# RWKV stage of a two-block model: both pairs of heads taken through every stage together, with smaller buffers beside it

## The chip, the cores and the metric

The kernel runs on one core of one Trainium2 chip. The metric is the device time of one execution in microseconds (us); before the change it was 2177.82 us as the median of three runs (2176.29 to 2183.47).

## The reference, cut to what matters

The program computes two transformer-like blocks. The first takes x (512 tokens, 1024 channels), norms it, projects it to four mixers of 256 channels (forgetting attention "fox", stick-breaking attention "stick", RWKV-7 time mix, gated linear recurrence "lru"), scales each by the silu of a gate, multiplies by an output matrix and adds the result to x. The second block has two layers whose norms are modulated by columns computed from a condition vector (`silu(c) @ w_ada + b_ada`).

The RWKV mixer has four heads of 64 channels. In the reference it is a scan over tokens:

```
def step(state, inp):
    r_t, w_t, k_t, v_t, kk_t, a_t = inp
    sa = jnp.einsum('bhij,bhj->bhi', state, -kk_t)
    state = (state * w_t[:, :, None, :]
             + sa[..., None] * (kk_t * a_t)[:, :, None, :]
             + v_t[..., None] * k_t[:, :, None, :])
    return state, jnp.einsum('bhij,bhj->bhi', state, r_t)
...
y = ((y - mean) * lax.rsqrt(var + GN_EPS)).reshape(b, s, G) * ln_g + ln_b
bonus = jnp.sum(r * k * r_k, axis=-1, keepdims=True) * v
return y + bonus.reshape(b, s, G)
```

## The kernel before, in words

Engines: TensorE (PE) multiplies, VectorE (DVE) and ScalarE (ACT) work on vectors, GpSimd (POOL) helps, SyncE (SP) issues the DMAs. All of them work through their own instructions in a fixed order.

**First block.** `first_block` (L403) norms x and splits the result into two float32r parts hH and hL (one buffer each, L389 to L393), which all projections read. A chunk of weights is loaded as raw tile `wr` (three buffers of 128x1024, 512 KB), copied by ACT to `wh` (L149) and subtracted by DVE to `wl` (L150); two buffers each. `proj_a` (L167) then makes three matmuls per step of 128 channels (L178, L179, L182). The steps are traced in the order of `B_ORDER`: `sq` (q, k, v of stick), `rw` (all of RWKV), `st` (stick), `fq` (q, k, v of fox), `lr`, three gates, `ad` (the modulation columns of the first layer, `ada`, L926), `fo` (fox, L523) and `g0`, the gate of fox.

**RWKV.** `rwkv` (L572) projects r, k, v and the low-rank features, and calls `rwkv_pair` (L635) for heads 0 and 1, then for heads 2 and 3. A pair computes operands, their transposes, Gram matrices over four blocks of 128 tokens (L731), the inverse of a triangular matrix by six doublings (`prod`, L756 to L783; each doubling of a head is three products of eight small matmuls, L761, with a copy and two subtractions of DVE between), parts that don't depend on the state, four state steps (L819 to L846) and a group norm. Its single-buffer tiles (`ar`, `gb`, `gk`, `up`, `cu`, `cl`) make the second pair wait for the first.

**Modulation columns.** `ada` multiplies 12 groups of 512 outputs by two vectors: 96 loads of 256 KB into tiles `wa` of their own (four buffers), four matmuls each (L938), and per group one copy to `row` (ACT), one transpose by the identity (PE) and one add (DVE, L945). The group's PSUM bank `ad` is single.

**After the mixers.** `out_split` (L1138) splits the mixers' output y into hH and hL again, in the very buffers that held the parts of x, and multiplies (L1154 to L1156). The second block follows, with tables of rope loaded into tiles `rcs` and `rsn` in the memory that the first block's working tiles held.

**What sets the order.** The framework orders each engine's instructions when the program is built: code traced earlier has priority, an instruction takes a place as soon as the framework's own estimate sees its inputs and a free buffer, and lower priorities fill the gaps. The lanes `rw`, `at`, `qkv`, `wa` have as many buffers as `B_LANES` says.

```
B_LANES = dict(rw=18, at=5, qkv=9, wa=4)
```

Of the kernel before, what the change touches and what calls it, by code (L numbers as in the profile page):

```python
# [16 lines left out]
P = 128  # L17
D = 1024
# [24 lines left out]
B_LANES = dict(rw=18, at=5, qkv=9, wa=4)  # L43
# [27 lines left out]
class Stream:  # L71
    """A run of n tokens (the latents or the context) with its buffers."""
# [7 lines left out]
class Kern:  # L80
# [41 lines left out]
    def t2(self, n=512):  # L122
        """A [128, n <= 512] float32 working tile of the current lane."""
# [29 lines left out]
    def weights(self, dram, nk):  # L153
        """Two halves of the chunk, each (H, L)."""
# [89 lines left out]
    def rstd_small(self, ss, scale, eps, post=1.0):  # L244
        """ss: SBUF [128, m]; returns post * (ss*scale + eps)^-1/2."""
# [10 lines left out]
    def consts(self):  # L256
        """What the scalar engine's tables are needed for comes first."""
# [8 lines left out]
        # 8 softplus(-lambda) of the recurrence, negated: 8 (ln sigmoid|lambda| - max(-lambda, 0))  # L266
# [6 lines left out]
        # silu of the conditioning vectors, as 32 columns  # L273
# [32 lines left out]
    def add_sq(self, s, k, key="ss", scale=1.0, first=None):  # L306
        """Adds the squares of channel tile k, scaled, to a sum of the stream's."""
# [8 lines left out]
    def mean_sq(self, s, sums):  # L316
        """Mean over the channels + eps, of each token: [128, token tile]."""
# [8 lines left out]
    def spread(self, s, r):  # L326
        """[128, token tile] to one row of all tokens on every partition."""
# [38 lines left out]
    def xy(self, s):  # L366
        """The residual stream and the mixers' output take turns in one buffer."""
# [15 lines left out]
    def res(self, s, d):  # L383
        """The residual of channel tile d, read back."""
# [15 lines left out]
# ======================================================================================  # L400
# first block
# ======================================================================================
    def first_block(self, s, con, filler):  # L403
        nc, a = self.nc, self.a
        with self.phase("b1", dict(rw=3, at=2, ad=1), B_LANES):
# [12 lines left out]
            steps = dict(rw=self.rwkv, ad=filler, fq=lambda: v.update(f=self.qkv(0, 1, 2)), fo=lambda: self.fox(v["f"]),  # L418
                         sq=lambda: v.update(s=self.qkv(4, 5, 6)), st=lambda: self.stick(v["s"]), lr=self.lru,
# [4 lines left out]
        # output projection and residual, with the norm of the context beside it  # L424
# [56 lines left out]
    def gates(self, which):  # L481
        """Scales rows of y by silu of the gate projections."""
# [8 lines left out]
    def qkv(self, cq, ck, cv):  # L491
# [12 lines left out]
    def flip(self, p, nk, tag):  # L504
        """[q, keys] -> [keys, (kt) q]."""
# [7 lines left out]
    def pv_pair(self, pts, vals, g, out, grid=None, tag="at"):  # L513
        """out [(head, d), q] of heads 2g and 2g+1 from their weights [keys, (kt) q]."""
# [57 lines left out]
    def rwkv(self):  # L572
# [7 lines left out]
        # triangular masks [128, 2, 128]; of the diagonal's 64 blocks [128, 64]: per level, and the identity  # L580
# [7 lines left out]
        lora = self._ld(work, "lora", [P, 2 * G])  # L588
# [13 lines left out]
        def ev_low(j, s, acc):  # L602
# [3 lines left out]
            else:  # L606
                # forget gates: cumulative log sigmoid, negated, as two float32r rows per head
# [27 lines left out]
    def rwkv_pair(self, hp, r, k, v, low, lora, gmask, lmask):  # L635
        nc = self.nc
        work = self.work
        col = lambda key: self.col1(key, hp)
        t4 = lambda t: t.rearrange("p (b t) -> p b t", b=4)
        big = lambda tag, dt=F32, bufs=1: work.tile([P, 8, P], dt, name=self.nm(tag), tag=tag, bufs=bufs)  # L640

        # removal key
# [6 lines left out]
        # 1/sqrt(max(ss, 1e-12))  # L649
# [4 lines left out]
        # decay: log decay = -exp(-1/2) sigmoid(w0 + tanh(wl) w2), cumulated within each block  # L654
# [29 lines left out]
        # replacement key  # L684
# [6 lines left out]
        # bonus  # L691
        bon = self.t2()
# [5 lines left out]
        # operands with the decays folded in  # L698
        ar = work.tile([P, 4, 2, P], F32, name=self.nm("ar"), tag="ar", bufs=1)
# [8 lines left out]
        # token-major copies  # L708
# [8 lines left out]
        tk = lambda key, h, b: tok[key][:, b * P + h * 64 : b * P + h * 64 + 64]  # L717

        # Gram matrices [s, t] by (head, block): beta.alpha (s<t), beta.rho, kappa.alpha (s<t), kappa.rho
        gb = work.tile([P, 8, 2, P], F32, name=self.nm("gb"), tag="gb", bufs=1)  # L720
        gk = big("gk")
        z = self.t2().rearrange("p (b h i) -> p b h i", b=4, h=2)
        gm = lambda n: gmask.rearrange("p (o a) t -> p o a t", o=1).to_broadcast([P, n, 2, P])
        for h in range(2):
            c = slice(h * 64, h * 64 + 64)
            ga = t4(self.t2())
            for src in (be, ka):
                for b in range(0, 4, 2):
# [4 lines left out]
                    u = slice(4 * h + b, 4 * h + b + 2)  # L733
                    if src is be:
                        nc.vector.tensor_tensor(gb[:, u], g, gm(2), ALU.mult)
                    else:
                        for o, m in ((ga[:, b : b + 2], 0), (gk[:, u], 1)):
                            nc.vector.tensor_tensor(o, g[:, :, m], gmask[:, m : m + 1].to_broadcast([P, 2, P]),
                                                    ALU.mult)
# [1195 lines left out]
```

## Time and profile before

| | |
|---|---|
| runs shown, median (lowest to highest) | 2177.82 us (2176.29 to 2183.47) |
| profiled execution, first to last instruction | 2176.9 us; the page gives no time around it |
| PE busy, share of the span | 2058.9 us, 95% |
| DVE, ACT, POOL busy | 1296.8, 993.4, 189.3 us |
| DMA | 221.95 MB, 102 GB/s over the span |
| mean granted clock of PE | 0.976 |

Matmuls are pipelined, so a busy PE is not a PE at its peak; and an engine's idle time matters only where nothing else holds the end. The first block ends where the first L1154 starts, at 395.89 us.

### The profile page before, as it was taken

What the parts mean: (1) busy time and instruction counts of PE and PEld (TensorE: products, weight loads), DVE (VectorE), ACT (ScalarE), POOL (GpSimd) and SP (SyncE); (2) the same over time, 40 slices, a digit from 0 to 9 for tenths busy, and PEclk for the clock granted to TensorE, in tenths of its full rate; (3) what the DMA queues carried; (4) which work ended last, traced back from release to release, by engine and by line L of the source; (5) the groups of instructions that cost most, each with busy time, mean ns of one, the idle gap of its engine ahead of it and who ended that gap; (6) DMA issues with size and microseconds to landing.
All of it is one profiled execution on the core that took longest, in us unless ns stands there. A gap on an engine that the chain in (4) does not pass through costs nothing.

```text
span 2176.9 us, 31989 instructions
## 1 busy us (share of the span) xinstructions
PE 2058.9 (95%) x12676; PEld 1669.3 (77%) x12676; DVE 1296.8 (60%) x2279; ACT 993.4 (46%) x1875; POOL 189.3 (9%) x148
## 2 busy tenths in 40 slices
PE   7999999978999899899999999989988989999999
PEld 5877766778957766788888888879957757787887
DVE  5354453676645575768885444677665656554544
ACT  4343743544756854542231323455656644242432
POOL 1011010032001000600000000161010001000000
PEclk9999999988999999999999999999999999999999
DMA  6323344332101124335673112434211222232232
GB/s 221 120 69 108 103 123 131 114 102 78 49 25 59 59 88 159 117 96 158 218 228 103 60 49 97 129 116 131 81 35 54 76 91 70 89 100 92 79 115 87
DMA packets 87622, 221.95 MB, mean 102 GB/s; under 512 B 13744, under 2 KB 24752, under 8 KB 87344
## 3 DMA queue, kind: packets, MB, share of 16 engines
q1 hardware_dynamic: 87472, 219.90, 31.6%
q8 instruction: 100, 1.64, 0.3%
q14 instruction: 50, 0.41, 0.1%
HBM read 212.53 MB, written 7.34 MB: 101 GB/s over the span
## 4 chain that ended last, share of the span: by engine, by line
PE 75%; DVE 13%; ACT 5%; DMA 4%; issue 2%; SPq 0%; POOL 0%; DVEq 0%; ACTq 0%; POOLq 0%
PE ps L178 15%; PE ps L182 14%; PE ps L179 14%; PE ps L203 3%; PE ps L202 3%; PE ps L204 3%; DVE wl L150 2%; DMA wr<-in_wadaT 2%; PE ps L1417 2%; PE ps L1154 2%; PE ps L1155 2%; PE ps L1156 2%; PE ps L397 2%; PE ps L1408 1%; PE ps L519 1%
## 5 line engine op out<-in xcount | busy, mean ns | idle before, releaser
L178 PE MATMUL ps<-hH,wh 128*128 128x512 f32 (+1 forms) x1424 | 511.2, 364 | 14.9 <-ACT wh L149 12.1
L179 PE MATMUL ps<-hL,wh 128*128 128x512 f32 (+1 forms) x1424 | 499.5, 360 | 1.4 <-DVE hL L363 0.7
L149 ACT CAST wh<-wr 128x1024 fp32r<-128x1024 f32 (+4 forms) x302 | 284.2, 943 | 464.1 <-PE ps L179 380.4
L150 DVE TENSOR_TENSOR wl<-wr,wh 128x1024 fp32r<-128x1024 f32 (+4 forms) x266 | 288.2, 1086 | 254.3 <-ACT wh L149 243.6
L182 PE MATMUL ps<-hH,wl 128*128 128x512 f32 (+1 forms) x1248 | 430.9, 369 | 2.8 <-DVE wl L150 2.8
L178 PEld LDWEIGHTS ps<-hH,wh 128*128 128x128 f32 x1424 | 271.5, 191 | 68.0 <-ACT wh L149 13.5
L179 PEld LDWEIGHTS ps<-hL,wh 128*128 128x128 f32 x1424 | 271.6, 191 | 43.6 <-issue 1.9
L182 PEld LDWEIGHTS ps<-hH,wl 128*128 128x128 f32 x1248 | 222.1, 188 | 39.5 <-DVE wl L150 4.8
L203 PE MATMUL ps<-wl,hH 128*128 128x256 f32 x704 | 203.2, 290 | 12.3 <-DVE wl L150 12.3
L202 PE MATMUL ps<-wh,hH 128*128 128x256 f32 x704 | 203.4, 291 | 0.2 <-ACT wh L149 0.2
L204 PE MATMUL ps<-wh,hL 128*128 128x256 f32 x704 | 200.6, 287 | 0.0
L178 PE MATMUL ps<-uH,wh 128*128 128x512 f32 (+1 forms) x528 | 187.7, 362 | 6.3 <-ACT uH L149 4.0
L179 PE MATMUL ps<-uL,wh 128*128 128x512 f32 (+1 forms) x528 | 181.6, 357 | 0.4 <-DVE uL L150 0.4
L182 PE MATMUL ps<-uH,wl 128*128 128x512 f32 (+1 forms) x488 | 155.4, 365 | 1.5 <-DVE wl L150 1.3
L203 PEld LDWEIGHTS ps<-wl,hH 128*128 128x128 f32 x704 | 137.4, 195 | 15.6 <-DVE wl L150 14.4
L202 PEld LDWEIGHTS ps<-wh,hH 128*128 128x128 f32 x704 | 136.7, 195 | 4.3 <-issue 2.9
L204 PEld LDWEIGHTS ps<-wh,hL 128*128 128x128 f32 x704 | 136.4, 195 | 1.0 <-issue 0.7
L1660 DVE SCALAR_TENSOR_TENSOR xy<-ps,mod,xy 128x512 f32<-128x512 f32 (+1 forms) x96 | 60.8, 658 | 128.1 <-PE ps L182 124.9
L150 POOL TENSOR_TENSOR wl<-wr,wh 128x1024 fp32r<-128x1024 f32 (+1 forms) x36 | 84.1, 2342 | 605.8 <-ACT wh L149 598.1
L178 PEld LDWEIGHTS ps<-uH,wh 128*128 128x128 f32 x528 | 99.4, 189 | 33.2 <-ACT wh L149 7.2
L179 PEld LDWEIGHTS ps<-uL,wh 128*128 128x128 f32 x528 | 99.7, 189 | 16.0 <-DVE uL L150 0.8
L145 ACT COPY t<-ps 128x512 f32<-128x512 f32 (+4 forms) x127 | 61.9, 490 | 89.7 <-PE ps L397 34.3
(364 smaller groups left out, 3276.4 us busy)
## 6 DMA issues: line engine op xcount, KB each, us to landing
wr<-in_up SPq DMA_DIRECT2D x110, 512.0 KB, 3.5
wa<-in_wada SPq DMA_DIRECT2D x96, 256.0 KB, 3.2
wr<-in_wadaT SPq DMA_DIRECT2D x48, 512.0 KB, 4.3
wr<-in_win2b SPq DMA_DIRECT2D x36, 512.0 KB, 3.5
wr<-in_win SPq DMA_DIRECT2D x30, 512.0 KB, 3.8
wr<-in_dn SPq DMA_DIRECT2D x40, 320.0 KB, 2.9
wr<-in_dn SPq DMA_DIRECT2D x32, 384.0 KB, 3.1
wr<-in_wout SPq DMA_DIRECT2D x12, 512.0 KB, 4.0
```

Source lines behind the costliest of these rows:

```text
L145: self.nc.any.tensor_copy(out, in_)
L149: self.nc.scalar.copy(hi, src)
L150: (eng or self.nc.vector).tensor_tensor(lo, src, hi.bitcast(F32), ALU.subtract)
L178: nc.tensor.matmul(acc[s], wh, fh(k), start=(q == 0), stop=False)
L179: nc.tensor.matmul(acc[s], wh, fl(k), start=False, stop=False)
L182: nc.tensor.matmul(acc[s], wl, fh(k), start=False, stop=(q == nk - 1))
L202: nc.tensor.matmul(bank[:, i], fh(k), wh, start=start, stop=False)
L203: nc.tensor.matmul(bank[:, i], fh(k), wl, start=False, stop=False)
L204: nc.tensor.matmul(bank[:, i], fl(k), wh, start=False, stop=stop)
L397: self.nc.tensor.transpose(out, in_, self.ident[:k, :k])
L1154: nc.tensor.matmul(acc, wh, yH[:, k], start=(q == 0), stop=False)
L1660: nc.vector.scalar_tensor_tensor(s.x[:, d, :], acc, self.mcol(5, d, s), s.x[:, d, :], ALU.mult, ALU.add)
```

## The change

RWKV no longer runs pair after pair. `rwkv_pair` is cut into `rwkv_operands`, `rwkv_gram`, `rwkv_inverse`, `rwkv_free`, `rwkv_block` and `rwkv_finish`, and each stage is traced for both pairs before the next; a doubling goes over four heads. To hold that, `ar` gets two buffers and `gb` four, and the lane `rw` 29 tiles in place of 18 tiles and several special ones. Space comes from elsewhere: the q of both attentions lies in rows of the output y that the mixer fills later, the bonus in y as well, the lane `qkv` falls from nine tiles to five and `at` from five to four, and `ada` loads its weights into the raw weight tiles `wr`, two steps of k at a time (48 loads of 512 KB), which it shares with all projections. What is computed stays the same.

```diff
-B_LANES = dict(rw=18, at=5, qkv=9, wa=4)
+B_LANES = dict(rw=29, at=4, qkv=5)
...
-        qt, kt, v = ([self.t2() for _ in range(2)] for _ in range(3))
+        kt, v = ([self.t2() for _ in range(2)] for _ in range(2))
+        qt = [self.y[:, row + j, :] for j in range(2)]
...
-        for hp in range(2):
-            self.rwkv_pair(hp, fs["r", hp], fs["k", hp], fs["v", hp], low["t"], lora, gmask, lmask)
...
+        pairs = [dict(hp=hp, r=fs["r", hp], k=fs["k", hp], v=fs["v", hp]) for hp in range(2)]
+        for d in pairs:
+            self.rwkv_operands(d, low["t"], lora)
+        for d in pairs:
+            self.rwkv_gram(d, gmask)
+        self.rwkv_inverse(pairs, lmask)
+        for d in pairs:
+            self.rwkv_free(d)
+        for b in range(4):
+            for d in pairs:
+                self.rwkv_block(d, b)
+        for d in pairs:
+            self.rwkv_finish(d)
...
-        bon = self.t2()
+        bon = self.y[:, 4 + hp, :]
...
-        for l in range(6):
-            for h, us in enumerate(hs):
+            for gb, up, cuh, clh, gd in heads:
...
-            for k in range(KT):
-                w = self.work.tile([P, 512], F32, name=self.nm("wa"), tag="wa", bufs=self.lanes["wa"])
-                self.dma(w, a["wada"][g, k])
-                for j in range(4):
+            for k0 in range(0, KT, 2):
+                w = self.wtile("wr")
+                self.dma(w.rearrange("p (k c) -> p k c", k=2), a["wada"][g, k0 : k0 + 2].rearrange("k p c -> p k c"))
+                for i in range(2):
+                    k = k0 + i
+                    for j in range(4):
```

Before, SP's queue in the middle of the first block reads as follows; `wr<-in_win` is a chunk of projection weights, `wa<-in_wada` one of modulation weights.

```order
L138 DMA wa_3014<-in_wada 128x512
L138 DMA wr_2330<-in_win 128x1024
L138 DMA wr_2388<-in_win 128x1024
L138 DMA wa_3020<-in_wada 128x512
L138 DMA wa_3026<-in_wada 128x512
L138 DMA wr_2394<-in_win 128x1024
L138 DMA wr_2452<-in_win 128x1024
L138 DMA wa_3032<-in_wada 128x512
```

In the changed program SP's queue holds no modulation weights until the weights of `g6`, the last gate but one, are issued; the place where they begin is this.

```order
L138 DMA wr_2728<-in_win 128x1024
L138 DMA wr_2790<-in_win 128x1024
L138 DMA wr_2796<-in_win 128x1024
L138 DMA wr_2862<-in_wada 128x2x512
L138 DMA wr_2872<-in_wada 128x2x512
L138 DMA wr_2882<-in_wada 128x2x512
L138 DMA t_3838<-in_xT 128x512
L138 DMA t_3860<-in_xT 128x512
```

From here on 48 loads of `in_wada` stand in a row, broken only by reads of x (`in_xT`), and the gate `g0`'s weights come behind the last of them. Before, they were spread from the start of the block to its end.

On PE, the end of the first block was this before: the last state step of pair 2 (L844), the last fox head's transposes (L397) and products (L519), then the output matrix (L1154).

```order
L844 MATMUL ps_1997<-sn_1983,ar_1442 128x128
L397 MATMUL ps_3835<-ident,t_3831 128x128 x4
L519 MATMUL ps_3842<-t_3822,t_2322 64x128
L519 MATMUL ps_3842<-t_3840,t_2322 64x128
L519 MATMUL ps_3842<-t_3822,t_2322 64x128
L519 MATMUL ps_3842<-t_3840,t_2322 64x128
L519 MATMUL ps_3842<-t_3822,t_2323 64x128
L519 MATMUL ps_3842<-t_3840,t_2323 64x128
L519 MATMUL ps_3842<-t_3822,t_2323 64x128
L519 MATMUL ps_3842<-t_3840,t_2323 64x128
L1154 MATMUL ps_3941<-hH_3925,wh_3936 128x512
L1155 MATMUL ps_3941<-hL_3926,wh_3936 128x512
```

In the changed program the fox heads (L521 is now their product) stand between modulation matmuls (L968 is the former L938), and the gate `g0` (L178, L179) comes last; one piece of it:

```order
L968 MATMUL ps_3367<-wr_3388,sc 32x128 x8
L397 MATMUL ps_3719<-ident,t_3715 128x128 x4
L521 MATMUL ps_3726<-t_3706,t_2302 64x128
L968 MATMUL ps_3367<-wr_3398,sc 32x128 x8
L521 MATMUL ps_3726<-t_3724,t_2302 64x128
L521 MATMUL ps_3726<-t_3706,t_2302 64x128
L521 MATMUL ps_3726<-t_3724,t_2302 64x128
L521 MATMUL ps_3726<-t_3706,t_2303 64x128
L521 MATMUL ps_3726<-t_3724,t_2303 64x128
L521 MATMUL ps_3726<-t_3706,t_2303 64x128
L521 MATMUL ps_3726<-t_3724,t_2303 64x128
L397 MATMUL ps_3410<-ident,row_3408 128x128
```

The 48 matmuls of `g0`, which read hH and hL of x, follow this last row directly, and the output matrix follows them. Before, `g0` stood between the Gram matrices and doublings of pair 2. From the first modulation matmul to the last the matmuls of 23 loads stand in front of the row where the last state step of RWKV ends, and those of 25 behind it.

DVE's order at the same hand-over was this before: L488 is `g0`'s gate on y, L150 with hL the split of y, L439 the first sums of the output matrix.

```order
L488 TENSOR_TENSOR xy_207<-xy_207,t_3889 128x512
L858 TENSOR_REDUCE sm_2010<-t_2008 128x8
L488 TENSOR_TENSOR xy_207<-xy_207,t_3917 128x512
L150 TENSOR_TENSOR hL_3926<-xy_207,hH_3925 128x512
L249 TENSOR_SCALAR sm_2012<-sm_2010 128x8
L150 TENSOR_TENSOR hL_3926<-xy_207,hH_3925 128x512
L439 TENSOR_TENSOR xy_207<-t_3954,ps_3941 128x512
```

In the changed program the same place on DVE reads:

```order
L488 TENSOR_TENSOR xy_207<-xy_207,t_3773 128x512
L150 TENSOR_TENSOR wl_3843<-wr_3841,wh_3842 128x512
L488 TENSOR_TENSOR xy_207<-xy_207,t_3801 128x512
L150 TENSOR_TENSOR hL_3810<-xy_207,hH_3809 128x512 x8
L1320 TENSOR_TENSOR rcs_4276<-rcs_4276,sm_4273 128x4x32
L1323 TENSOR_TENSOR rsn_4277<-rsn_4277,sm_4273 128x4x16 x2
L439 TENSOR_TENSOR xy_207<-t_3838,ps_3825 128x512
```

All eight splits of y now follow the last gate, where five of them came long before it, and the rope table `rcs` stands in front of the first sum.

## Rows read from the trace of the kernel before

**Rows 1.** Stretches of the block: busy time of each engine, then clock, DMA share, GB/s.
```profile
core 0: us, PE busy (x) PEld busy (x) DVE busy (x) ACT busy (x) POOL busy (x), PEclk, DMA share, GB/s
0.00:20.00 20.00, 4.94 (x36) 4.37 (x40) 9.97 (x29) 11.08 (x19) 1.69 (x11) 1.00 0.90 316
20.00:396.00 376.00, 367.36 (x3356) 273.38 (x3345) 176.47 (x338) 170.58 (x312) 35.89 (x49) 1.00 0.35 110
...
376.00:396.00 20.00, 17.45 (x117) 12.42 (x115) 7.65 (x21) 8.25 (x19) 0.00 (x0) 0.93 0.00 1
396.00:425.00 29.00, 26.78 (x116) 21.01 (x117) 23.98 (x51) 18.49 (x36) 2.66 (x1) 0.99 0.61 176
```

**Rows 2.** PE's waits, 155 to 396 us: total, times, longest.
```profile
PE ps L938 <- DMA wa<-in_wada: 2.3, 5, 0.8
PE ps L397 <- DVE t L542: 1.9, 2, 1.5
PE ps L830 <- DVE u L825: 1.6, 2, 1.2
```

**Rows 3.** PE in order of time, behind the first norm: start, us, what.
```profile
18.93 2.20 PE L938 MATMUL ps<-wa,sc 128*32 128x128 f32 x32
...
31.95 0.64 PE L938 MATMUL ps<-wa,sc 128*32 128x128 f32 x14
```

**Rows 4.** PE in order of time, modulation matmuls among pair 2's doublings.
```profile
338.27 0.43 PE L938 MATMUL ps<-wa,sc 128*32 128x128 f32 x8
...
346.16 0.85 PE L938 MATMUL ps<-wa,sc 128*32 128x128 f32 x20
```

**Rows 5.** DMA issues: count, KB each, median us to landing.
```profile
wa<-in_wada SPq DMA_DIRECT2D x96, 256.0 KB, 3.2
...
wr<-in_win SPq DMA_DIRECT2D x30, 512.0 KB, 3.8
```

**Rows 6.** Chain of waits, second block, the other layer's modulation weights on two buffers.
```profile
1047.37 4.64 DMA wr<-in_wadaT
...
1055.68 4.47 DMA wr<-in_wadaT
```

**Rows 7.** PE in order of time, last fox heads; idle time before in brackets.
```profile
382.93 1.09 PE L519 MATMUL ps<-t,t 128*64 128x128 f32 x14
...
388.04 0.63 PE L397 MATMUL ps<-ident,t 128*128 128x128 f32 x4 [0.44 <-DVE t L542]
388.60 1.12 PE L532 MATMUL ps<-t,t 64*128 64x512 f32 x2
389.65 0.50 PE L534 MATMUL ps<-cumr,sm 128*128 128x512 f32 x1
```

**Rows 8.** ACT and DVE by line, 390 to 426 us: count, busy, mean ns.
```profile
L149 ACT CAST wh<-wr 128x1024 fp32r<-128x1024 f32 x2 | 2.1, 1050 | 1.5 <-PE ps L1155 1.5
L149 ACT CAST hH<-xy 128x512 fp32r<-128x512 f32 x3 | 1.9, 628 | 2.2 <-DVE xy L488 2.2
L486 ACT ACTIVATE t<-ps 128x512 f32<-128x512 f32 x2 | 1.1, 594 | 0.0
...
L488 DVE TENSOR_TENSOR xy<-xy,t 128x512 f32<-128x512 f32 x3 | 2.1, 688 | 1.8 <-ACT t L486 1.8
L150 DVE TENSOR_TENSOR hL<-xy,hH 128x512 fp32r<-128x512 f32 x3 | 2.1, 687 | 0.0
```

**Rows 9.** ACT by line, 20 to 400 us: the modulation's copy.
```profile
L145 ACT COPY row<-ps 128x128 f32<-128x128 f32 x11 | 2.9, 264 | 6.3 <-PE ps L938 6.3
```

**Rows 10.** Chain of waits, 402 to 416 us: start, us, what.
```profile
402.96 0.23 PE ps L1155
...
406.13 0.70 DVE xy L866
...
409.71 4.62 DMA rcs<-in_rope
```

**Rows 11.** PE's longest wait, 396 to 425 us.
```profile
PE ps L1154 <- DVE xy L444: 0.9, 1, 0.9
```

More of the change, by code (lines that the diff above doesn't have):

```diff
@@ L762, in prod @@
             return out
-        gd = [work.tile([P, 4, 64], F32, name=self.nm("gd"), tag="gd", bufs=2) for _ in range(2)]
-        hs = [slice(0, 4), slice(4, 8)]
-        for h, us in enumerate(hs):
-            for q in halves:
-                nc.gpsimd.tensor_copy(gd[h][q], gb[q, us, 0, q])
+        heads = []
+        for d in pairs:
+            cu, cl, gd = two(), two(), two()
+            d["up"] = [t4(self.t2()) for _ in range(2)]
+            for h in range(2):
+                nc.gpsimd.memset(d["up"][h][64:128, :, 0:64], 0.0)
+                for q in halves:
+                    nc.gpsimd.tensor_copy(gd[q, h], d["gb"][h][q, :, 0, q])
+                heads.append((d["gb"][h], d["up"][h], cu[:, h], cl[:, h], gd[:, h]))
         for l in range(6):
-            for h, us in enumerate(hs):
-                cuh, clh = cu[:, us], cl[:, us]
-                an = half()
-                nc.gpsimd.tensor_tensor(an, gd[h], c4(lmask[:, l : l + 1]), ALU.mult)
+            for gb, up, cuh, clh, gd in heads:
+                an, xx = (t[:, i] for t in (two(),) for i in range(2))
+                nc.gpsimd.tensor_tensor(an, gd, c4(lmask[:, l : l + 1]), ALU.mult)
                 if l == 0:
@@ L785, in rwkv_pair @@
         lo, hi = halves
-        for h, us in enumerate(hs):
+        for gb, up, cuh, clh, _ in heads:
             for q in halves:
-                nc.gpsimd.tensor_copy(up[q, us, q], cu[q, us])
+                nc.gpsimd.tensor_copy(up[q, :, q], cuh[q])
             xp = self.ps([P, 4, 64], "rw")
             for b in range(4):
-                nc.tensor.matmul(xp[hi, b], gb[lo, 4 * h + b, 0, hi], cl[lo, 4 * h + b], start=True, stop=True)
-            xx = half()
+                nc.tensor.matmul(xp[hi, b], gb[lo, b, 0, hi], clh[lo, b], start=True, stop=True)
+            xx = two()[:, 0]
             self.copy(xx[hi], xp[hi])
@@ L808, in rwkv_pair @@
             for b in range(4):
[L809 to L818 removed]
+                nc.tensor.matmul(atp[h * 64 : h * 64 + 64, b], tk("al", h, b), up[h][:, b], start=True, stop=True)
@@ new lines, in rwkv_free, with rwkv_block @@
+        d["at"] = self.t2().rearrange("p (b t) -> p b t", b=4)
+        nc.scalar.activation(d["at"], atp, AF.Copy, scale=-1.0)
+        d["yt"] = self.t2()
+    def rwkv_block(self, d, b):
+        nc, work = self.nc, self.work
+        tok, tk, fac, st, u0 = d["tok"], d["tk"], d["fac"], d["st"], d["u0"]
+        y4 = d["yt"].rearrange("p (b h i) -> p b h i", b=4, h=2)
+        if st is None:
+            u = u0[:, 0]
+        else:
+            upz = self.ps([P, 2, 64], "rw")
+            nc.tensor.matmul(upz, d["at"][:, b, :], st, start=True, stop=True)
+            u = work.tile([P, 2, 64], F32, name=self.nm("u"), tag="u", bufs=3)
+            nc.vector.tensor_tensor(u, u0[:, b], upz, ALU.add)
+        if b < 3:
+            s = slice(b * P, (b + 1) * P)
+            sp = self.ps([P, P], "rw")
+            nc.tensor.matmul(sp, tok["be"][:, s], u, start=True, stop=False)
+            nc.tensor.matmul(sp, tok["ka"][:, s], tok["v"][:, s], start=False, stop=True)
+            sn = work.tile([P, P], F32, name=self.nm("sn"), tag="sn", bufs=5)
@@ L838, in rwkv_pair @@
-            yp = self.ps([P, 2, 64], "rw")
-            for h in range(2):
-                un = 4 * h + b
-                nc.tensor.matmul(yp[:, h], gk[:, un], tk("v", h, b), start=(h == 0), stop=False)
-                nc.tensor.matmul(yp[:, h], gb[:, un, 1, :], u[:, h], start=False, stop=(h == 1 and st is None))
-            if st is not None:
-                nc.tensor.matmul(yp.rearrange("p h i -> p (h i)"), ar[:, b, 1, :], st, start=False, stop=True)
-            nc.scalar.copy(y4[:, b], yp)
@@ L846, in rwkv_pair @@
-            st = sn
+                nc.vector.tensor_tensor(sn, st, sp, ALU.add)
+                nc.vector.scalar_tensor_tensor(sn, sn, fac[:, b : b + 1], self.hsum, ALU.mult, ALU.mult)
+            d["st"] = sn
+        yp = self.ps([P, 2, 64], "rw")
+        for h in range(2):
+            nc.tensor.matmul(yp[:, h], d["gk"][h][:, b], tk("v", h, b), start=(h == 0), stop=False)
+            nc.tensor.matmul(yp[:, h], d["gb"][h][:, b, 1, :], u[:, h], start=False, stop=(h == 1 and st is None))
@@ L849, in rwkv_pair, with rwkv_finish @@
+        if st is not None:
+            nc.tensor.matmul(yp.rearrange("p h i -> p (h i)"), d["ar"][:, b, 1, :], st, start=False, stop=True)
+        nc.scalar.copy(y4[:, b], yp)
+    def rwkv_finish(self, d):
+        nc, hp, yt = self.nc, d["hp"], d["yt"]
+        col = lambda key: self.col1(key, hp)
         y8 = yt.rearrange("p (g i) -> p g i", i=64)
@@ L870, in lru @@
         self.lane = "n"
-        lw = self._ld(self.work, "lruw", [P, 4 * P])
-        ho = {}
+        lw = self.t2()
+        self.dma(lw, a["lruw"])
         def ev(j, s, acc):
```

96 lines of the change are left out of this document (40 added, 56 removed).

## The prediction

> **What bounds the kernel now.** I read the stretches first, to see whether an engine or a wait holds the first block. From 20 to 396 us PE is busy 367.36 of 376 us, DVE 176.47, ACT 170.58, and the DMA engines run at 0.35 [rows 1]. So PE bounds the block and idles 8.6 us in it. Before 20 us it is DMA: PE is busy 4.94 of 20 us while the transfers run at 0.90 and 316 GB/s. I then asked what PE waits for. Of the 8.6 us, 2.3 wait for modulation weights, 1.9 for the fox softmax (L542) and 1.6 for the state step's `u` (L825) [rows 2]. The state steps stand at the end, in 376 to 396, where PE is busy 17.45 of 20 us at a granted clock of 0.93 on the mean (1.00 is 2.4 GHz, so a part of it went at 1.2). The rest of the span is the second block; in its later part PE's order is the same row by row in both programs, so I give it 0 with ±3.
>
> The time to win is therefore small by construction: at most the 8.6 us of idle time and what fewer switches between kinds of matmul save. The time to lose is larger, because PE has no slack: every wait that the new order brings is paid in full.
>
> **The change part by part.** All sums are made against the profiled execution, whose span is 2176.9 us; the page gives no time around it, and the median of the runs shown, 2177.82 us, stands 0.9 us above it.
>
> (a) Waits that four heads at once can fill. The doublings and state steps of one pair now have the other pair's beside them, so the 1.6 us for `u` should go, and the 2.3 us for modulation weights move elsewhere (counted in d). Some of L542's waits may be filled too. What is late next there is the copy and the two subtractions between the products, of four heads now, and DVE has room. I take -4.5; bounds 0 (the waits come back elsewhere) and -8.6 (all idle time gone).
>
> (b) Fewer runs of modulation matmuls. Eight records take 0.43 us and twenty 0.85 [rows 4], so a record costs 0.035 and a run 0.15 by itself. A run is a stretch of them broken by other matmuls; PE's order has 63 before and 40 after. 23 x 0.15 = -3.5; bounds 0 and -4.6 (0.2 each).
>
> (c) The modulation matmuls leave the start. Behind the first norm PE ran four such runs, eight loads in all, for 3.9 us (the first 2.20 us at 18.93, the last 0.64 at 31.95) [rows 3]. The first filled a hole while DVE made hL. They cost PE about 2 us less where they hid, and are paid elsewhere: +2; bounds 0 and +4.
>
> (d) The loads. Before, 96 loads of 256 KB had four buffers of their own and came one by one between weights. Now 48 loads of 512 KB go through the three raw weight buffers, and SP issues none before `g6`'s weights; then they stand in a row. A 512 KB load lands in 3.8 us, a 256 KB one in 3.2 [rows 5], so bytes come cheaper, but a buffer is refilled only when PE has read it. The other layer's modulation already works that way with two buffers: a load issued at a release at 1047.37 lands 4.64 us later, and the same place of the cycle comes round only at 1055.68 [rows 6]. With three buffers and PE ready at once, a load costs (4.64 + 0.71)/3 = 1.8 us, where 0.71 is 16 records by (b); by the bandwidth of the start it is 0.524 MB / 316 GB/s = 1.7 [rows 1]. With the cycle of 8.31 it is 2.8. Behind the last state step stand 25 loads, 25 x 1.8 = 45 us, three of them fetched early: 40. PE's work beside them is 25 x 0.71 = 18 us of modulation, seven fox rows of heads of 0.56 + 1.05 + 0.50 = 2.1 us (start to start, the last by its duration) and four sets of products of 1.09 [rows 7]: 18 + 15 + 4 = 37 us. So on the mean the loads lag by 3 us, and where three loads' matmuls stand in a row, PE uses three buffers in 2.1 us and waits for the next; I add 4 for that. +7. Bounds: 0 (the 23 loads before the last state step run ahead, and the mean covers all) and 25 x 2.8 - 3 x 2.8 - 37 = +25.
>
> The Trainium skill ("DMA: Bandwidth & Descriptors", Rules for kernel authors) advises large transfers, 1 MiB or more for the highest bandwidth, and an early issue with a late wait so that the setup is hidden. The first half agrees with rows 5 (half the bytes cost 3.2 us, all of them 3.8) and by it the term would be 0 and the sum 7 us smaller; the second half speaks against this change, whose loads are issued late and waited for soon. I follow rows 6, where such a queue is seen to wait.
>
> (e) Between two groups stands a copy of `row` (264 ns [rows 9]), a transpose and an add, on a single bank. Before, other work stood between; now in four places the transposed row follows the matmuls directly, and the next group waits for the bank. The copy and two hand-overs are some 1 us each: 4 x 1 = +4; bounds 0 and +8.
>
> (f) `g0`'s weights (SP) come behind the last modulation load, so its first chunk lands 3.8 us after a buffer is free [rows 5], and the cast on ACT takes 1.05 [rows 8]. Its 48 matmuls follow PE's last transpose directly; fox's products and last loads cover most: +1.5; bounds 0 and +4.
>
> (g) The hand-off to the output matrix. `g0` is now last, and all eight splits of y follow it: Silu 0.594, product 0.688, cast 0.628, subtract 0.687 [rows 8], 2.6 us from the last `g0` matmul to the last hL, in front of the first L1155 that needs it. Before, three splits were late too, and PE idles 2.2 us in 396 to 425 [rows 1], the longest wait 0.9 [rows 11]. Behind the splits DVE now has the rope table `rcs`, in front of the first sum. Its load is issued when the block's tiles are freed: before, DVE's release ended at 406.83, the rcs load was issued behind other issues at 409.71 and took 4.62 [rows 10], 7.5 us in all. If the sums wait on DVE behind it, PSUM banks run out and PE stops. The 7.5 us have 8 splits of 0.69 and some 10 us of the output matrix beside them; I take +3.5, bounds -2 (the old waits go and nothing comes) and +8.
>
> (h) Granted clock. Where PE waits, it had 0.93 in 376 to 396 with 87% busy [rows 1]. The modulation stretch is of that kind and twice as long: 37 us x 0.07 = 2.6, less the 1.4 of the old stretch, with some room: +2; bounds 0 and +10 (half of R3's).
>
> Sum: -4.5 - 3.5 + 2 + 7 + 4 + 1.5 + 3.5 + 2 = +12. Span 2176.9 + 12 = 2188.9, and with the 0.9 that the median stands above the span, **2190 us**. DVE's and ACT's work hardly changes in count and hides under PE. A difference of up to 0.3% (6.5 us: 2171.3 to 2184.3) can't be told from no change here.
>
> **Rivals.** R1, the loads are covered: terms d to h are near zero, as the 23 loads ahead of the last state step suggest, since during them PE has a good deal of other work; a and b cancel c and the rest. For it: DMA share is 0.00 in 376 to 396 [rows 1], so bandwidth is free just there. Against: three buffers for everything. -8 + 2 + 4 + 2 = 0: 2178.
>
> R2, faster: the same, and the four chains fill the waits wholly: -8.6 - 4.6 + 2 + 2 = -9: 2169. For it: idle time in [rows 2] is just of waits for DVE. Against: it is only 8.6 us in all, and (c) and (g) must stay small.
>
> R3, a bound by the loads with a clock at half: in the last stretch every load costs 2.8 us and PE waits in front of most runs. The upper end of term d, +25; the stretch's 37 us and `g0`'s 11 (48 x 0.23, by the 0.23 that a step of L1155 takes in the chain [rows 10]) need up to twice their time at 1.2 GHz, 48 more, of which the load waits hide most; I take 10. The other terms sum to about 0: 2212. It decides from 2.2 us a load on. For it: rows 6 and the 0.93. Against: SP runs ahead of PE during the doublings.
>
> The Trainium skill ("TensorE: Matmul & The Clock Gate", HAM oscillation) says that slices whose compute is shorter than the wait for the next one's weights fall back to the low clock each time. By it the stretch would go the way of R3; the 0.93 with 17.45 of 20 us busy points the same way, weakly, and no stretch of this trace shows such a queue on PE.
>
> **How the numbers follow.** The forecast 0.55 (its own range 2182 to 2204: from d, g and h at their low ends to d at 15 and h at 5), R1 0.20, R2 0.15, R3 0.10. R2 lies almost wholly below 2171.3, and a little of R1: faster 0.17. Most of R1 and the low edge of the forecast lie within: same 0.23. Slower 0.60. The range runs from R2's near edge to R3: 2171 to 2214, which leaves out half of R2 and part of R3.
>
> **What would show it.** (a) is right if PE no longer waits for `u` L825's counterpart; (b) if modulation busy time falls from 38 us a few; (d) if PE waits for `wr` of `in_wada` by 5 to 10 us in the last 50 us of the block, R1 if under 2, R3 if over 25; (e) if PE's row transposes wait for the ACT copy some 0.5 us each; (f) and (g) if the first L1154 starts some 8 us later than 395.89 and L439's sums wait for the `rcs` load; (h) by the granted clock of the block's last 50 us. I am wrong at the root if the block's end moves earlier, or if the second block moves by more than 3 us.

## The result and the profile after

| | before | after |
|---|---|---|
| median (lowest to highest) | 2177.39 us (2176.29 to 2183.47) | 2205.38 us (2201.88 to 2214.59) |
| ratio, 95% interval | 1 | 1.0115 [1.008, 1.0149] |
| profiled execution, span | 2176.9 us | 2200.1 us |
| start of the first output matmul (L1154; after: L1185) | 395.89 us | 418.04 us |
| PE idle from 20 us to there | 8.6 us | 30.4 us |
| from there to the end | 1781.0 us | 1782.1 us |

The change makes the kernel 0.8 to 1.5% slower (the ratio is estimated from all runs; it is not the quotient of the two medians). Of the 23.2 us between the two spans, 22.15 arise before the first output matmul; the second block takes what it took.

The stretches of the changed kernel (time, PE, PEld, DVE, ACT and POOL busy, granted clock, DMA share, GB/s), to be read against [rows 1]:

```profile
core 0: us, PE busy (x) PEld busy (x) DVE busy (x) ACT busy (x) POOL busy (x), PEclk, DMA share, GB/s
0.00:20.00 20.00, 3.94 (x16) 3.56 (x16) 11.24 (x39) 11.16 (x20) 1.11 (x10) 1.00 0.88 303
20.00:418.00 398.00, 367.63 (x3372) 278.05 (x3372) 175.00 (x329) 170.27 (x315) 39.41 (x53) 0.97 0.31 104
...
153.50:167.20 13.70, 9.01 (x30) 5.91 (x29) 7.97 (x10) 11.10 (x18) 2.84 (x3) 0.50 0.00 1
...
418.00:447.00 29.00, 27.17 (x110) 21.28 (x111) 22.77 (x46) 18.36 (x34) 0.00 (x0) 0.94 0.62 184
```

PE works as long as before (367.63 us, 367.36 before); the stretch is 22 us longer because PE waits in it. For 13.7 us from 153.5 on it runs at 1.2 GHz (0.50). PE's waits in the same stretch (total, times, longest), against [rows 2]:

```profile
PE ps L968 <- DMA wr<-in_wada: 8.3, 10, 1.5
PE ps L711 <- DVE xy L709: 4.7, 1, 4.7
PE ps L397 <- DVE t L568: 3.1, 2, 1.6
PE ps L968 <- DVE mod L976: 3.1, 3, 2.6
PE ps L397 <- ACT row L145: 2.8, 4, 1.1
PE ps L178 <- ACT hH L149: 2.1, 1, 2.1
PE ps L179 <- DVE hL L150: 1.4, 1, 1.4
...
PE ps L397 <- DVE t L544: 0.9, 2, 0.7
```

Three places. At the start, PE in order of time; the 2.20 us of modulation work of [rows 3] no longer stand in the hole that hH and hL leave:

```profile
21.00 1.22 PE L178 MATMUL ps<-hH,wh 128*128 128x512 f32 x2 [2.11 <-ACT hH L149]
23.67 0.80 PE L179 MATMUL ps<-hL,wh 128*128 128x512 f32 x1 [1.45 <-DVE hL L150]
```

In the middle is a hole that the kernel before did not have: the projections pause (the last starts at 149.18, the next at 194.85; before, they paused from 165 to 197 beside pair 1's matmuls), and pair 2's operands aren't ready (L709 is the bonus, L711 its sum over channels, L568 a product of stick). PE, then ACT:

```profile
151.10 0.41 PE L397 MATMUL ps<-ident,t 128*128 128x128 f32 x2 [1.64 <-DVE t L568]
...
158.32 2.07 PE L711 MATMUL ps<-xy,hsum 128*128 128x512 f32 x2 [4.69 <-DVE xy L709]
```

```profile
151.94 1.28 ACT L1925 ACT_TABLE_LOAD   x1
153.24 0.21 ACT L689 ACTIVATE sm<-sm 128x4 f32<-128x4 f32 x1
...
154.02 0.80 ACT L704 ACTIVATE t<-t,sm,cols 128x512 f32<-128x512 f32 x1
154.84 1.28 ACT L1925 ACT_TABLE_LOAD   x1
```

The chain behind L709 goes through ACT and DVE, with ACT changing its function table for 1.28 us between RWKV's functions and stick's. L711 itself takes 2.07 us, at 1.2 GHz. Before, the same two records took 1.12 us behind a wait of 0.59 and behind other work:

```profile
288.41 0.39 PE L182 MATMUL ps<-hH,wl 128*128 128x512 f32 x1
288.73 0.85 PE L938 MATMUL ps<-wa,sc 128*32 128x128 f32 x22
290.18 1.12 PE L695 MATMUL ps<-t,hsum 128*128 128x512 f32 x2 [0.59 <-DVE t L693]
```

At the end the modulation loads. The page's issues (KB each, median us to landing), the chain of waits, and all the modulation matmuls together:

```profile
wr<-in_wada SPq DMA_DIRECT2D x48, 512.0 KB, 4.3
```

```profile
384.12 4.25 DMA wr<-in_wada
389.20 4.14 DMA wr<-in_wada
394.09 5.35 DMA wr<-in_wada
```

```profile
L968 PE MATMUL ps<-wr,sc 128*32 128x128 f32 x768 | 33.8, 291 | 11.5 <-DMA wr<-in_wada 8.3 <-DVE mod L976 3.1
```

A load that the chain waits for lands 4.1 to 5.4 us after its buffer came free, as in [rows 6]. The hand-over to the output matrix, on DVE and in the chain, against [rows 10]:

```profile
418.23 4.90 DVE L150 TENSOR_TENSOR hL<-xy,hH 128x512 fp32r<-128x512 f32 x8
425.44 0.29 DVE L1320 TENSOR_TENSOR rcs<-rcs,sm 128x128 f32<-128x128 f32 x1 [2.32 <-DMA rcs<-in_rope]
...
426.01 0.68 DVE L439 TENSOR_TENSOR xy<-t,ps 128x512 f32<-128x512 f32 x1
```

DVE does wait 2.32 us for the rope table in front of the first sum, but PE loses only 1.8 us from 418 to 447 (2.2 before).

### The profile page after: what moved, and what is told of

The parts are those of the page before. It is cut to its first block, busy times and chain, and to the rows that moved or that the text cites. A ratio compares the mean times of both kernels' runs of the same rounds, so it can differ in the third digit from the quotient of the medians.

```text
span 2200.1 us, 31908 instructions
## 1 busy us (share of the span) xinstructions
PE 2055.0 (93%) x12676; PEld 1670.2 (76%) x12676; DVE 1296.5 (59%) x2278; ACT 992.8 (45%) x1875; POOL 190.9 (9%) x150
## 3 DMA queue, kind: packets, MB, share of 16 engines
q8 instruction: 100, 1.64, 0.3%
## 4 chain that ended last, share of the span: by engine, by line
PE 73%; DVE 13%; ACT 5%; DMA 5%; issue 2%; POOL 0%; SPq 0%; POOLq 0%; DVEq 0%; ACTq 0%
PE ps L178 15%; PE ps L182 14%; PE ps L179 14%; PE ps L203 3%; PE ps L204 3%; PE ps L202 3%; DMA wr<-in_wadaT 2%; DVE wl L150 2%; PE ps L1448 2%; PE ps L1185 2%; PE ps L1186 2%; PE ps L1187 2%; PE ps L397 2%; PE ps L1439 1%; DMA wr<-in_wada 1%
## 5 line engine op out<-in xcount | busy, mean ns | idle before, releaser
L178 PE MATMUL ps<-hH,wh 128*128 128x512 f32 (+1 forms) x1424 | 510.8, 364 | 17.1 <-ACT wh L149 11.4
L179 PE MATMUL ps<-hL,wh 128*128 128x512 f32 (+1 forms) x1424 | 498.1, 360 | 2.2 <-DVE hL L150 1.4
L150 DVE TENSOR_TENSOR wl<-wr,wh 128x1024 fp32r<-128x1024 f32 (+4 forms) x266 | 288.2, 1086 | 265.3 <-ACT wh L149 255.8
L178 PEld LDWEIGHTS ps<-hH,wh 128*128 128x128 f32 x1424 | 271.7, 191 | 69.8 <-ACT wh L149 13.0
L179 PEld LDWEIGHTS ps<-hL,wh 128*128 128x128 f32 x1424 | 272.1, 191 | 44.1 <-DVE hL L150 2.2
L203 PE MATMUL ps<-wl,hH 128*128 128x256 f32 x704 | 203.9, 291 | 12.6 <-DVE wl L150 12.5
L202 PE MATMUL ps<-wh,hH 128*128 128x256 f32 x704 | 203.4, 291 | 1.6 <-ACT wh L149 1.4
L204 PE MATMUL ps<-wh,hL 128*128 128x256 f32 x704 | 201.5, 289 | 0.3 <-DVE hL L363 0.3
L178 PE MATMUL ps<-uH,wh 128*128 128x512 f32 (+1 forms) x528 | 187.6, 362 | 6.8 <-ACT uH L149 4.6
L179 PE MATMUL ps<-uL,wh 128*128 128x512 f32 (+1 forms) x528 | 181.1, 357 | 0.4 <-DVE uL L150 0.4
L202 PEld LDWEIGHTS ps<-wh,hH 128*128 128x128 f32 x704 | 137.3, 196 | 5.1 <-ACT wh L149 1.9
L204 PEld LDWEIGHTS ps<-wh,hL 128*128 128x128 f32 x704 | 137.5, 196 | 1.0 <-DVE hL L363 0.5
L150 POOL TENSOR_TENSOR wl<-wr,wh 128x1024 fp32r<-128x1024 f32 (+1 forms) x36 | 83.8, 2334 | 600.7 <-ACT wh L149 593.3
L178 PEld LDWEIGHTS ps<-uH,wh 128*128 128x128 f32 x528 | 99.3, 189 | 33.6 <-ACT wh L149 7.4
L179 PEld LDWEIGHTS ps<-uL,wh 128*128 128x128 f32 x528 | 99.6, 189 | 15.9 <-DVE uL L150 0.8
```

Source lines behind the costliest of these rows:

```text
L178: nc.tensor.matmul(acc[s], wh, fh(k), start=(q == 0), stop=False)
L179: nc.tensor.matmul(acc[s], wh, fl(k), start=False, stop=False)
L202: nc.tensor.matmul(bank[:, i], fh(k), wh, start=start, stop=False)
L203: nc.tensor.matmul(bank[:, i], fh(k), wl, start=False, stop=False)
L204: nc.tensor.matmul(bank[:, i], fl(k), wh, start=False, stop=stop)
```

## The experiments

Every run has two marks from its trace: the first output matmul, and what the expectations call the end of the output matrix, which is the start of its 96th of 192 matmuls (422.2 us before, 444.6 after). "Rest" is the span behind the second mark. The kernel before had medians of 2178.3 to 2179.6 us beside these runs. Half clock is the time granted at 1.2 GHz between 20 us (or the start) and the first output matmul, by the record of the granted clock; before 2.5 us, after 20.5.

| run | median us | ratio [95%] | first output | 96th | idle | half clock | rest |
|---|---|---|---|---|---|---|---|
| before | 2177.4 | 1 | 395.9 | 422.2 | 8.6 | 2.5 | 1754.7 |
| after | 2205.4 | 1.0115 [1.0080, 1.0149] | 418.0 | 444.6 | 30.4 | 20.5 | 1755.5 |
| e1 before + shared ring | 2211.7 | 1.0131 [1.0107, 1.0154] | 409.6 | 438.0 | 21.1 | 17.1 | 1776.3 |
| e2 after, 4 own tiles, rw 25 | 2224.8 | 1.0201 [1.0177, 1.0224] | 388.0 | 453.4 | 17.9 | 10.2 | 1764.5 |
| e3 after, rw 25 | 2207.4 | 1.0125 [1.0106, 1.0143] | 419.5 | 447.6 | 28.1 | 27.3 | 1759.2 |
| e4 after, ad behind fq | 2188.5 | 1.0040 [1.0025, 1.0054] | 396.8 | 423.0 | 14.0 | 9.7 | 1761.8 |
| e5 after, 2 own tiles, rw 27 | 2233.3 | 1.0253 [1.0223, 1.0284] | 399.5 | 457.2 | 12.3 | 17.1 | 1772.9 |
| e6 after, ad behind st | 2249.5 | 1.0335 [1.0310, 1.0359] | 451.7 | 477.6 | 47.8 | 74.6 | 1768.9 |
| e7 pairs in turn, own tiles | 2190.6 | 1.0057 [1.0037, 1.0077] | 394.4 | 434.0 | 10.0 | 3.4 | 1751.4 |
| e8 half the bytes | 2210.3 | 1.0154 [1.0132, 1.0177] | 415.2 | 441.6 | 26.3 | 26.8 | 1764.7 |
| e9 e4 + pairs in turn | 2203.7 | 1.0125 [1.0103, 1.0147] | 401.1 | 431.7 | 14.7 | 10.2 | 1765.6 |
| e10 after, ad behind lr | 2183.0 | 1.0025 [1.0012, 1.0037] | 390.8 | 418.4 | 11.1 | 6.8 | 1765.8 |
| e11 after, Gram 1 early | 2233.2 | 1.0243 [1.0208, 1.0279] | 444.0 | 472.3 | 29.9 | 78.5 | 1766.1 |
| e12 e11 + ad behind lr | 2191.0 | 1.0049 [1.0031, 1.0068] | 402.3 | 431.1 | 15.0 | 17.1 | 1758.4 |

The rest differs by up to 25 us between kernels that have the same second block in their code. The framework orders it anew for each (behind the second mark PE's order is that of the changed kernel in e3 and e12 alone), and the clock differs too. So theories on the first block are judged by the marks, and the times beside them. Each mark is of one execution; how much it varies between executions was not measured.

**e1: the shared ring alone, in the kernel before.**

```diff
-                w = self.work.tile([P, 512], F32, name=self.nm("wa"), tag="wa", bufs=self.lanes["wa"])
-                self.dma(w, a["wada"][g, k])
+                w = self.wtile("wr")
+                self.dma(w.rearrange("p (k c) -> p k c", k=2), a["wada"][g, k0 : k0 + 2].rearrange("k p c -> p k c"))
```

> The kernel before with one part of the change alone: the modulation weights go as 48 loads of 512 KB through the three raw weight tiles; pairs of heads stay one after the other. Theory T1 (the shared ring: a tile of it is given out in the order of the code, so the modulation matmuls can no longer start before g6's weights and no longer fill PE's holes early in the block): nearly the whole loss is here, 15 to 25 us over the kernel before, 2192 to 2203, with the first output matmul at 411 to 420 us. Rival T2 (four heads at once: the operand chains of both pairs lie bare): only the late waits for loads and for the row copy stay, 12.9 us of the profile after less the 2.3 of before, so +8 to +12, 2185 to 2190.

Measured 2211.7; the first output at 409.6, 13.7 us late, the 96th mark 15.8 late. T2's +8 to +12 is too little, T1's 411 to 420 a little too much, and the time is over both because the rest took 22 us more, which neither theory speaks of. PE's waits up to 410:

```profile
PE ps L940 <- DMA wr<-in_wada: 6.5, 10, 1.1
PE ps L397 <- DVE t L566: 3.6, 4, 1.5
PE ps L178 <- ACT hH L149: 2.1, 1, 2.1
...
PE ps L397 <- ACT row L145: 1.7, 4, 0.4
PE ps L940 <- DVE mod L948: 1.3, 5, 0.3
```

The first modulation matmul now starts at 267.8 us (18.93 before), and the last at 391.3. The start's hole and the late loads are here; a wait of 4.7 us for the bonus is not. So this part alone costs the block some two thirds of what the change costs it, and the middle hole comes only with the rest of the change. The shares don't simply add: e1 has 17.1 us at 1.2 GHz from 382.7 on, among its modulation loads, where the changed kernel has 6.8 us of it.

**e2 and e3: own tiles back; its control.**

```diff
-B_LANES = dict(rw=29, at=4, qkv=5)
+B_LANES = dict(rw=25, at=4, qkv=5, wa=4)      # e2, with ada as before; e3: rw=25 alone
```

> The changed kernel with the modulation weights back in four tiles of their own (96 loads of 256 KB), for whose space the lane rw gives up four tiles (25). Theory T1: the fillers are back, the waits of 149 to 158 us and of the late loads go: 2168 to 2182, as the kernel before or a little under it. Rival T2: the operand chains keep their 6 us of waits and the 5 us at half clock: 2187 to 2195.

> The changed kernel with 25 tiles in the lane rw in place of 29, nothing else: the control for the run with own tiles. Both theories: as the changed kernel, 2198 to 2210; a gain or loss over 8 us would say that the size of the lane matters by itself.

e3 measured 2207.4, as expected: four tiles of rw matter little while other work is late too. The middle hole is there again (4.7 us for the bonus, 13.7 us at 1.2 GHz from 152.8 on). e2 measured 2224.8 and speaks for neither. Idle time before the first output fell to 17.9 us and no L711 wait is left, but then RWKV's four state steps ran behind fox, and the output matrix waited for them. e2's stretches:

```profile
400.00:420.00 20.00, 18.86 (x129) 16.86 (x128) 8.23 (x21) 3.45 (x9) 0.00 (x0) 1.00 0.19 53
420.00:440.00 20.00, 7.95 (x31) 5.31 (x31) 12.19 (x24) 6.59 (x13) 2.65 (x1) 0.60 0.06 20
```

From 420 to 440 PE does 8 us of work at 0.60. The holes at the front went, and one at the end came: what ends last lies bare.

**e4: the modulation step earlier in the code, nothing else.**

```diff
-B_ORDER = "sq rw st fq lr g4 g2 g6 ad fo g0"
+B_ORDER = "sq rw st fq ad lr g4 g2 g6 fo g0"
```

> The changed kernel with the modulation step traced right behind fox's q, k and v, ahead of the recurrence and the gates; tiles as in the change. Theory T1: the modulation matmuls can fill from the middle of the block and their loads no longer stand in one row: 8 to 15 us less than the changed kernel, 2190 to 2197. Rival T3 (three buffers for everything are the bound wherever the loads stand): the projections now wait for weights behind modulation loads instead, 2200 to 2215.

Measured 2188.5, below T1's 2190 to 2197: the second mark is 423.0, within 0.8 us of the kernel before, with the changed kernel's tiles, the same 48 loads and the same three buffers. T3 falls. PE's waits up to 397:

```profile
PE ps L521 <- ACT t L145: 4.2, 2, 3.3
PE ps L178 <- ACT hH L149: 2.1, 1, 2.1
PE ps L968 <- DMA wr<-in_wada: 2.1, 4, 0.8
...
PE ps L711 <- DVE xy L709: 0.8, 1, 0.8
```

The bonus wait went from 4.7 to 0.8 us and that for loads from 8.3 to 2.1. The modulation now runs from 143 to 291 us.

**e5: own tiles again, two of them.**

```diff
+B_LANES = dict(rw=27, at=4, qkv=5, wa=2)      # with ada as before
```

> The changed kernel with the modulation weights in two tiles of their own (96 loads of 256 KB) and 27 tiles in the lane rw: four heads at once, with fillers, and with less taken from rw than in the run with 25. Theory T1 (the shared ring took the fillers away): PE's idle time before the output matrix falls from 30.3 us to 8 to 14, half clock there from 20.5 us to under 8, the end of the block's output matrix comes at 418 to 428 us in place of 444.6, the time is 2172 to 2186. Rival T4 (whatever fills takes PE's time from RWKV's chain, which then ends last and lies bare, as with 25 tiles): the last state steps end behind the last fox head, the output matrix ends after 435, time over 2195.

Measured 2233.3. Of T1's signs only the idle time came, 12.3 us (first output at 399.5); half clock is 17.1 us, not under 8. T4's outcome came too, by another chain than it named: with two buffers the modulation itself ended last, at 443, among the output matrix. PE's waits from 396 to 460:

```profile
PE ps L966 <- DMA wa<-in_wada: 13.6, 9, 2.5
PE ps L321 <- DVE t L314: 8.3, 1, 8.3
```

The second row, the sums of a norm, was not followed up. Four heads with four tiles for modulation and 29 for RWKV stay untried: there is no room for both.

**e6: the step one earlier still** (`"sq rw st ad fq lr g4 g2 g6 fo g0"`).

> The changed kernel with the modulation step traced behind stick, ahead of fox's q, k and v: one step earlier than in the run with it behind them. Theory T1: earlier fillers, the last gate no longer last: end of the output matrix at 415 to 424 us, time 2172 to 2186. Rival T3 (three buffers for everything): the projections wait for their weights behind 48 loads: 2195 or more.

Measured 2249.5: far from T1, and in T3's range, but not by T3's mechanism. The projections waited only 1.3 us for weights; the work simply ran out, and fox's last heads stood alone at the end. The bonus wait is back too, at 3.6 us. Two stretches of e6:

```profile
300.00:387.00 87.00, 84.73 (x504) 68.87 (x504) 42.58 (x84) 50.11 (x85) 3.45 (x3) 1.00 0.16 52
387.00:452.00 65.00, 42.99 (x133) 21.71 (x134) 13.44 (x33) 15.25 (x36) 0.00 (x0) 0.50 0.00 1
```

For 65 us PE does nothing but fox, waits 22 us, and runs at 1.2 GHz throughout. T1's "the earlier the better" is wrong: fillers are a store that has to last to the end of the chains that leave holes.

**e7: what is left without both.**

```diff
-        for d in pairs:
-            self.rwkv_operands(d, low["t"], lora)
-        for d in pairs:
-            self.rwkv_gram(d, gmask)
...
+        for d in pairs:
+            self.rwkv_operands(d, low["t"], lora)
+            self.rwkv_gram(d, gmask)
+            self.rwkv_inverse([d], lmask)
...
+B_LANES = dict(rw=25, at=4, qkv=5, wa=4)
```

> The changed kernel with the pairs one after the other again and the modulation weights in four tiles of their own, rw 25: what is left of the change is where q, the bonus, lora and the pair's tiles lie, and the lanes. T1 and T2 alike: as the kernel before within 0.4%, 2172 to 2187; a loss over that would put the blame on the lanes or on q and bonus in the output buffer.

Measured 2190.6: first output 1.5 us earlier than before, the 96th 12 later, since pair 2's group norm (a wait of 5.3 us) stands among the output matmuls. The new lanes and places of q and bonus are thus not free, by somewhat more than expected; how much of it is the four tiles less is open.

**e8: half the bytes** (each load reads 256 KB, which both steps use; half of the weights are left out).

```diff
-                self.dma(w.rearrange("p (k c) -> p k c", k=2), a["wada"][g, k0 : k0 + 2].rearrange("k p c -> p k c"))
+                self.dma(w[:, 0:512], a["wada"][g, k0])
```

> The changed kernel with each of the 48 modulation loads cut to its first 256 KB, which both its steps then use (half the weights are left out); tiles, matmuls and their place stay. It parts the late stretch, where PE idles 8.3 us for modulation loads and 5.9 us for the row copy and the bank behind it. Theory D (the loads' landing through three buffers is the price there): waits for in_wada fall to under 3 us, the end of the output matrix moves from 444.6 to 434 to 440 us, time 2193 to 2200. Rival E (the chain of copy, transpose and add with one bank, and what it holds up): the waits for loads shrink but those for the row copy and the add stay or grow, end of the output matrix 441 or later, time over 2200.

Waits from 280 to 416:

```profile
PE ps L521 <- ACT t L145: 3.3, 1, 3.3
PE ps L178 <- ACT wh L149: 3.0, 1, 3.0
PE ps L968 <- DMA wr<-in_wada: 2.6, 4, 1.1
PE ps L397 <- ACT row L145: 1.6, 3, 0.7
...
PE ps L968 <- DVE mod L976: 1.4, 4, 0.6
```

Waits for loads fell by 5.7 us as D has it, but new ones of 6.3 us stand in the first two rows, and the mark moved by 3 us only (441.6, where E begins; the time is E's; e3, which differs from the changed kernel by four tiles alone, lies 3 us from it as well). Undecided between the two: the loads are a price of a few us, given back in part.

**e9: e4 with the pairs in turn** (the loops of e7, `ad` as in e4).

> The changed kernel with the modulation step behind fox's q, k and v and with the pairs of heads one after the other. Beside the run with that step there and four heads at once (2188, output matrix ended at 423.0 us) it prices the four heads alone. Theory F (four heads at once fill RWKV's waits and let it end before fox): this one is 6 to 12 us slower, output matrix ended at 429 to 435. Rival G (the order of heads is worth nothing once fillers lie beside it): 420 to 426, time 2181 to 2190.

Measured 2203.7, mark at 431.7: F by the mark; the time is 15.2 us over e4's, more than F's 6 to 12. Taking four heads together is worth 4.3 us at the first output and 8.6 at the 96th matmul, with fillers beside them.

**e10: the step between e4 and the change** (`"sq rw st fq lr ad g4 g2 g6 fo g0"`).

> The changed kernel with the modulation step one step later than in the good run, behind the recurrence, still ahead of the gates. Theory T5 (what counts is that fox's last heads have projections of the gates or modulation beside them, and that the early hole has a filler too): between the run with it behind fox's q, k and v (output matrix ended at 423.0) and the changed kernel (444.6): 424 to 434, time 2182 to 2194. Rival T3 (the shared buffers): as the changed kernel, 2200 or more.

Measured 2183.0, in T5's range, and the block is the best of all, better than T5's 424 to 434: first output at 390.8, 5.1 us earlier than before, 96th mark 418.4, 3.8 earlier. The rest takes 11 us more than before, so the kernel as a whole is still 0.25% slower. The interval leaves out no change, but the difference of 4.6 us is small beside the range of the kernel before in the same series (2170.62 to 2185.32).

**e11 and e12: pair 1's Gram matrices ahead of pair 2's operands,** alone and with e10.

```diff
         for d in pairs:
             self.rwkv_operands(d, low["t"], lora)
-        for d in pairs:
             self.rwkv_gram(d, gmask)
```

> The changed kernel with one thing back: the Gram matrices of the first pair are traced ahead of the second pair's operands; inverse, state steps and everything else stay with four heads. Theory H (the hole at 149 to 158 us, 6.3 us of waits for the second pair's operands and 13.7 us at 1.2 GHz behind it, comes from having no matmuls to put beside that chain, and the step was missing in my sum): the hole closes, the end of the output matrix moves from 444.6 to 432 to 437 us, time 2190 to 2197. Rival I (the hole is the price of the operand chain on ACT and DVE, which comes back later as a wait): 441 or later, 2199 or more.

> Both mends together, as the version that could beat both kernels: the first pair's Gram matrices ahead of the second pair's operands, and the modulation step behind the recurrence. PE's order of the second block is then that of the changed kernel row by row over most of its length. Theory: the first block as with the modulation step there alone or up to 5 us less (output matrix ended at 412 to 419 us), the second block as in the changed kernel (1755): time 2166 to 2177. Rival (the gap that the Gram matrices fill is filled by modulation already): 418 to 422, time 2174 to 2180.

e11 measured 2233.2, far off H; it is on I's side, and worse than I's bounds ask for. The hole came 17.5 us later (the bonus sum at 175.83 in place of 158.32), and what stood behind it was other work. PE in order of time, and two stretches:

```profile
168.78 0.87 PE L397 MATMUL ps<-ident,t 128*128 128x128 f32 x3 [5.36 <-DVE t L568]
...
175.83 2.08 PE L710 MATMUL ps<-xy,hsum 128*128 128x512 f32 x2 [2.27 <-DVE xy L708]
...
184.43 3.78 PE L751 MATMUL ps<-ar,t 64*128 64x256 f32 x8
```

```profile
168.00:180.00 12.00, 8.46 (x28) 4.68 (x29) 9.68 (x16) 7.12 (x12) 6.38 (x9) 0.50 0.00 1
...
200.00:210.00 10.00, 10.00 (x26) 6.47 (x27) 3.46 (x7) 1.49 (x4) 3.34 (x6) 0.50 0.00 0
```

Two waits, 7.6 us, and 47.8 us at 1.2 GHz from 167.6 on, with PE busy without a gap from 180 on. By half of PE's busy time in it that is a loss of some 22 us, an estimate. So H is not shown by this run. e12 measured 2191.0, mark 431.1, outside both of its ranges: 12.6 us worse than e10. It has a hole at the same place (10.2 us at 1.2 GHz from 167 on); how much of the 12.6 us comes from there was not parted. Neither beats the kernel before.

## Why the prediction was right and where it was not

Slower was right, and 2205.38 lies in the range, but outside the forecast's own (2182 to 2204): the first output was to come 8 us late and came 22.15 late. The range reached up to 2214 on account of R3, and R3 did not come; that the time lies in it is in part luck. By terms, from the waits above:

- (a) was forecast at -4.5 and is about +4.7. The wait for `u` went as forecast (1.6 us to none). But the step named the copy and the subtractions of the doublings as what is late next, and it is **the operands of pair 2**: 4.7 us for the bonus and 1.6 for a product of stick (L568), behind the same DVE and ACT queues. Before, pair 2's chain (273 to 290 us) lay beside the gates' projections, with 22 modulation matmuls last, and cost 0.6 us. The order showed that operands of both pairs now stand in a row; I priced only the stages where four heads help.
- (b) -3.5 against -4.9 (38.7 us of modulation busy time from 20 to 396 before, 33.8 now).
- (c) +2 against +3.7 (4.5 us of waits for hH, hL and the copy of q now, 0.8 before). But the step let the fillers matter only there. e4 and e10 show that they also close the middle hole: there the bonus wait is 0.8 us or none.
- (d) +7 against +6.0 (8.3 less 2.3; in the block's last 50 us 4.6, just under the 5 to 10 of the sign), (e) +4 against +5.9 (3.1 + 2.8), (f) +1.5 against 0.7: right within 2 us each. R3's 2.8 us a load did not come, nor R1's cover.
- (g) +3.5 against 1.5 for the first hH. DVE waits for the rope table as the step said, but PE loses no more than before from 418 to 447.
- (h) +2 against some +5: PE's busy time is as before although (b) took 4.9 off. The 13.7 us at 1.2 GHz alone, with 9.01 us busy, cost 4.5 by half of that (an estimate). They stand in and behind the hole of (a), not in the modulation stretch where I looked, which has 6.8 us at 1.2 GHz.

The terms sum to 22.6 beside the measured 22.15; as (h) is taken from PE's busy time, a part of this agreement is built in. The hole and the low clock in and behind it, 6.3 + 4.5 = 10.8 us, are what the forecast lacked.

The Trainium skill ("TensorE: Matmul & The Clock Gate", HAM oscillation) has slices whose compute is shorter than the wait for the next weights fall back to the low clock every time. In the modulation stretch of the changed kernel as a whole this condition is not met: from 351 to 404 us PE was busy 40.03 of 53 us in waits of at most 2.6 us, and the granted clock was 0.94. The trace of e1 agrees with it in one place. Three loads in a row are waited for longer than the 0.64 us that their matmuls took at full clock; the clock fell at 382.7 and stayed at 1.2 GHz for 17.1 us:

```profile
380.15 0.64 PE L940 MATMUL ps<-wr,sc 128*32 128x128 f32 x16 [1.13 <-DMA wr<-in_wada]
381.68 0.64 PE L940 MATMUL ps<-wr,sc 128*32 128x128 f32 x16 [0.89 <-DMA wr<-in_wada]
383.14 1.08 PE L940 MATMUL ps<-wr,sc 128*32 128x128 f32 x16 [0.82 <-DMA wr<-in_wada]
```

So the low clock that (h) looked for among the loads did come, in e1. In the changed kernel the longest spell is the one at 153.5.

What stays open: why the rest differs by up to 25 us where only the first block was edited, and what e10 would be worth with the rest of the kernel before. The clock has a part in it: behind the second mark 100.8 us were granted at 1.2 GHz before, 97.5 after, 111.7 in e10 and 138.6 in e1. If half of that time is lost, an estimate, it makes 19 of e1's 22 us and 5 of e10's 11. With the changed kernel's order of PE there, e3 and e12 lie 3.7 and 2.9 us over its rest.

## What to carry to other kernels

Work that depends on nothing is a filler only as long as its buffers are its own or its place in the code is early: in a shared ring, tiles are given out in the order of the code, and a step traced late starts late whatever its priority. Place such work by where the latency-bound chains leave holes, and spread it to the last of them: here one line that orders the steps was worth 27 us in the block (418.0 to 390.8), and one step too early cost 34. When stages of two chains are put side by side, price the stage that now comes first for both, not only those that overlap better.

## What the runs showed of the hardware

Two holes of like size had very different prices. In the changed kernel PE waited 1.64 and 4.69 us; the granted clock fell at 153.5, just ahead of the second wait, and was at 1.2 GHz for 13.7 us. It came back among transposes over 128 rows that ran without a gap. In e11 the waits were 5.36 and 2.27 us; the clock fell at 167.6, within the first, and was at 1.2 GHz for 47.8 us, though from 180 us on PE was never idle. Until 211 it worked there on products over 64 rows (L751, L559), transposes and some small products over 128 rows (L521, L761), and the clock rose 4 us after projections (L202 to L204) had begun again. What kept it low was not tried. A change of ACT's function table cost 1.28 us of ACT here, and the next instruction began 0.02 us later (151.94 to 153.24).
